# Mamba-2 layer of a two-layer trunk: the step-size chain's stacked operand is written in place, and the hold on group 0's convolutions starts later in the group and ends later in the chain

## The chip, the cores and the metric

The kernel runs on one core of one Trainium2 chip. TensorE (PE, the matmuls), VectorE (DVE), ScalarE (ACT), GpSimd (POOL) and SyncE (SP, which here only issues transfers) each work through a queue of their own in order. An instruction that must wait for another engine holds up everything behind it in its queue. The metric is the device time of one execution in microseconds.

## The reference, cut to what matters

The step runs a gated-MLP layer, a Mamba-2 layer and an MLP after each, on 256 prompt rows and 8 sequences of 8 rows (320 columns in the kernel). The change lies in the Mamba-2 mixer:

```python
zxbcdt = h @ w_in                                  # 6144 columns and 32 for dt
conv = conv_b + xp[:, 0:l] * conv_w[0]
for k in range(1, CONV_W):
    conv = conv + xp[:, k:k + l] * conv_w[k]
xbc_c = jax.nn.silu(conv)                          # gives x, B, C
dt = jax.nn.softplus(dt_raw + dt_bias)             # 32 heads
a = -jnp.exp(a_log)
...
acum = jnp.cumsum(dt * a, axis=2)                  # within a chunk
seg = acum[:, :, :, None] - acum[:, :, None, :]
decay = jnp.exp(jnp.where(causal, seg, -jnp.inf))
...
decay_to_end = jnp.exp(acum[:, :, -1:] - acum)
```

Every head needs `acum`, `dt` and `dt * decay_to_end` before its state-space work (the "ssd" below) can start.

## The kernel before, in words

Everything is feature-major: 128 partitions by 320 columns. Each projection tile (128 output features) takes 24 matmuls on PE: 8 blocks of the contraction, three products each (lines 307 to 309), since both operands are split into a high and a low part. A weight tile arrives by a transfer of SP's queue (`raw`, line 147), ACT makes its high part (`whi`, line 136) and DVE its low part (`wlo`, line 137). `whi` and `wlo` have three buffers each, so the fourth `whi` waits until PE has finished with the first. The results lie in three PSUM buffers, `mm`: a fourth tile can't start before ACT has read the first.

The Mamba-2 layer has eight groups. A group has six projection tiles: B, C, two tiles of x (here Xa, Xb) and two of the gate z (Za, Zb). B, C, Xa and Xb go through a convolution (`conv`): ACT copies the PSUM tile into `cb` (lines 640 and 641), POOL fills in and saves the borders (638, 639, 642, 643), ACT makes the first tap `co` (646), DVE adds the other three (649), and ACT applies Silu (651, 652). `cb` and `co` have three buffers each. Then comes the group's `ssd`: transposes and small matmuls on PE (lines 681 to 735), Y (757), the states (794), with the decay matrix `bc` made on ACT (687, 688) from rows that a transfer spreads over the partitions.

Ahead of group 0 stands the dt chain (lines 819 to 860), on the columns of `w_dt`, which are repeated four times over the partitions: softplus by a series on DVE (823 to 832), the running sum (835, 836), its exponentials on ACT (838, 841, 844), and a stacked operand `stk` whose four quarters of 32 partitions hold `acum`, `dt`, `dt` times the decay to the chunk's end, and `dt`. POOL writes `stk` in four instructions (845 to 848). PE transposes `stk` (854, 859) into `nat`, which every `ssd` needs, and SP writes `acum` and its exponential to DRAM (850, 851) and reads them back spread over the partitions (673, 674).

The order within each queue is set by a scheduler that runs when the kernel is built and that places instructions by costs of its own; the code's order is only a start. `tc.issue_after(i)` tells it that what stands under it must not be placed before `i`. With it, the three DVE taps of group 0's convolutions are held until the running sum (`dtl[0]`); `dtl` is cleared after group 0's convolutions, so later groups are never held. `widx` counts the projection tiles of the groups: within `conv` it is 1 for group 0's B, 2 for C, 3 for Xa, 4 for Xb.

Of the kernel before, what the change touches and what calls it, by code (L numbers as in the profile page):

```python
# [12 lines left out]
ADD, SUB, MUL, MIN, MAX = ALU.add, ALU.subtract, ALU.mult, ALU.min, ALU.max  # L13
# [9 lines left out]
T = TP + TS  # L23
# [22 lines left out]
C_ID, C_SS, C_S4, C_MASK, C_RST, C_DM, C_SEL, C_M = 0, 128, 138, 174, 494, 814, 1070, 1102  # L46
# [6 lines left out]
def tile_trunk(ctx: ExitStack, tc: tile.TileContext, io):  # L53
    nc = tc.nc
    pe, act, dve, pool = nc.tensor, nc.scalar, nc.vector, nc.gpsimd
# [12 lines left out]
    def nm(s):  # L68
        uid[0] += 1
        return f"{s}{uid[0]}"  # L70

    cst = const.tile([P, C_N], F32, name="cst")
# [546 lines left out]
    yst = [yp.tile([P, 8, T], F32, tag=f"yst{i}", name=f"yst{i}", bufs=1) for i in range(2)]  # L619
# [4 lines left out]
    widx = [0]  # L624
    dtl = []

    def in_tile():
        i = widx[0]
        widx[0] += 1
        if i < MG - 1:  # L630
            return scaled(pss[1 + i], r0)
        return proj_h(io["w_in"][i])

    def conv(ct, tag, bufs):
        ps = in_tile()
        cb = mb.tile([P, CW], F32, tag="cb", name=nm("cb"), bufs=3)
        cs = cb[:, 3 + TP :].rearrange("p (b t) -> p b t", t=11)
        pool.memset(cb[:, 0:3], 0.0)
        pool.tensor_copy(cs[:, :, 0:3], scv[:, ct])
        act.copy(cb[:, 3 : 3 + TP], ps[:, :TP])  # L640
        act.copy(cs[:, :, 3:], b1(ps[:, TP:T]))
        pool.tensor_copy(cvp[:, ct, :], cb[:, TP : TP + 3])
        pool.tensor_copy(scv[:, ct], cs[:, :, 8:])
        o = mb.tile([P, CW], F32, tag="co", name=nm("co"), bufs=3)
        wv = lambda k: vec[:, V_CW + ct * 4 + k : V_CW + ct * 4 + k + 1]
        act.activation(o[:, :CO], cb[:, :CO], AF.Identity, scale=wv(0), bias=vec[:, V_CB + ct : V_CB + ct + 1])  # L646
        with tc.issue_after(dtl[0]) if dtl else ExitStack():
            for k in range(1, 4):
                dve.scalar_tensor_tensor(o[:, :CO], cb[:, k : k + CO], wv(k), o[:, :CO], MUL, ADD)  # L649
        r = mb.tile([P, T], F32, tag=tag, name=nm(tag), bufs=bufs)  # L650
        act.activation(r[:, :TP], o[:, :TP], AF.Silu)
        act.activation(b1(r[:, TP:]), o[:, 3 + TP :].rearrange("p (b t) -> p b t", t=11)[:, :, 0:8], AF.Silu)
        return r
# [150 lines left out]
    def convs(g_, prev):  # L804
        B = conv(16 + g_, "Bt", 2)
        next(prev, None)
        C = conv(24 + g_, "Ct", 2)
        next(prev, None)
        X = []
        for r in range(2):  # L810
            X.append(conv(2 * g_ + r, "Xt", 4))
            next(prev, None)
        Z = mt([P, 2, T], "Z", 2)
        for r in range(2):
            act.activation(Z[:, r], in_tile()[:, :T], AF.Silu)
            next(prev, None)
        return B, C, X, Z

    raw, dt, acm, stk, t1, t2, t3 = (yst[1][:, i, :] for i in range(7))
    act.activation(raw, ps[:, :T], AF.Identity, bias=vec[:, V_DTB : V_DTB + 1])  # L820
    act.activation(t1, raw, AF.Abs)
    act.activation(t1, t1, AF.Exp, scale=-1.0)
# [10 lines left out]
    na = mb.tile([P, 1], F32, name="na")  # L833
    act.activation(na, vec[:, V_AL : V_AL + 1], AF.Exp)
    dve.tensor_scalar(t1, dt, na, -1.0, MUL, MUL)
    dtl.append(dve.tensor_tensor_scan(acm, cst[:, C_RST : C_RST + T], t1, 0.0, MUL, ADD).ins)
    eac = raw
    act.activation(eac, acm, AF.Exp)
    for c in range(2):
# [2 lines left out]
    a8 = b1(acm[:, TP:])  # L842
    dve.tensor_tensor(b1(t3[:, TP:]), a8[:, :, LS - 1 : LS].to_broadcast([P, NB, LS]), a8, SUB)
    act.activation(t2[:, TP:], t3[:, TP:], AF.Exp)
    pool.tensor_copy(stk[0:32], acm[0:32])
    pool.tensor_copy(stk[32:64], dt[32:64])
    pool.tensor_tensor(stk[64:96], dt[64:96], t2[64:96], MUL)
    pool.tensor_copy(stk[96:128], dt[96:128])
    rowd = dr.tile([2, NH, T], F32, name="rowd")
    nc.sync.dma_start(rowd[0], acm[0:32, :])  # L850
    nc.sync.dma_start(rowd[1], eac[0:32, :])
# [257 lines left out]
```

## Time and profile before

| | |
|---|---|
| median of 3 runs | 1079.7 us (1076.17 to 1083.86) |
| the profiled execution's own time | 1075.66 us |
| its span in the trace | 1073.9 us |
| mean granted TensorE clock | 0.986 of full speed |
| busy share: PE, DVE, ACT, POOL | 96%, 61%, 51%, 28% |
| dt chain's place in the span | 510 to 541 us |
| Mamba-2 groups' place in the span | 509 to about 790 us |

The span is shorter than the execution by 1.8 us. The busy shares are means over a span whose stages differ, so they say what the kernel is made of and not what a change in the dt chain is worth; for that one looks at the stretch in which the chain runs. The page divides the span into 40 slices of 26.8 us; slices 20 and 21 hold the chain.

### The profile page before, as it was taken

Reading aid. Unit: us, or ns where it says so; the run is one execution under the profiler, and the core shown is the slowest. Engines: PE = TensorE matmul, PEld = TensorE weight load, DVE = VectorE, ACT = ScalarE, POOL = GpSimd, SP = SyncE. Lnnn points to the kernel's source line nnn. Section 1 sums busy time; section 2 is a strip of 40 time slices with the busy share of each in tenths; the row PEclk is TensorE's granted clock in tenths of the full one; section 3 lists DMA queues with packets and bytes.
Section 4 is the critical chain, followed back from the end, with each engine's and each line's share of the span. In section 5 each row is a group of like instructions: output and inputs, shape, how many; then the busy total and the mean of one; then the engine's idle time right before and its main releaser. Section 6 shows DMA issues by size and latency. Waiting matters only on the chain.

```text
span 1073.9 us, 19747 instructions
## 1 busy us (share of the span) xinstructions
PE 1030.2 (96%) x7809; PEld 970.8 (90%) x7809; DVE 652.9 (61%) x1080; ACT 549.2 (51%) x1013; POOL 299.9 (28%) x403
## 2 busy tenths in 40 slices
PE   5999999999999999999688999999999999999996
PEld 3778998999999999999688999999999999999995
DVE  4545966437644443446968898898876754444432
ACT  4453343435644433335698777678345555543331
POOL 1200134332433311222123333532217243411001
PEclk9999999999999999999888999999999999999998
DMA  9957985775666667455435656565445544544431
GB/s 366 361 194 237 335 316 166 267 253 195 243 215 216 217 223 271 151 157 172 151 108 171 251 168 222 197 224 205 167 163 158 177 157 140 155 153 144 155 99 50
DMA packets 60877, 213.97 MB, mean 199 GB/s; under 512 B 6560, under 2 KB 12128, under 8 KB 58480
## 3 DMA queue, kind: packets, MB, share of 16 engines
q1 hardware_dynamic: 58544, 200.47, 55.1%
q0 software_dynamic: 1952, 11.98, 3.1%
q8 instruction: 61, 1.00, 0.4%
q10 hardware_dynamic: 288, 0.26, 0.1%
q14 instruction: 32, 0.26, 0.1%
HBM read 199.31 MB, written 12.85 MB: 198 GB/s over the span
## 4 chain that ended last, share of the span: by engine, by line
PE 76%; ACT 7%; DVE 6%; issue 5%; DMA 3%; POOL 2%; SPq 0%; POOLq 0%; ACTq 0%; DVEq 0%
PE mm L307 19%; PE mm L308 19%; PE mm L309 19%; PE adap L165 3%; ACT bc L687 2%; DMA bc<-rowd 2%; DVE wlo L137 2%; DVE co L649 2%; ACT whi L136 1%; PE mm L411 1%; PE mm L412 1%; PE mm L413 1%; PE ax L757 1%; DMA raw<-ada 1%; PE ax L307 1%
## 5 line engine op out<-in xcount | busy, mean ns | idle before, releaser
L137 DVE TENSOR_TENSOR wlo<-raw,whi 128x1024 fp32r<-128x1024 f32 (+1 forms) x243 | 298.1, 1228 | 203.5 <-ACT whi L136 202.6
L136 ACT ACTIVATE whi<-raw 128x1024 fp32r<-128x1024 f32 (+1 forms) x243 | 254.7, 1050 | 252.4 <-PE mm L308 195.0
L307 PE MATMUL mm<-hhi,whi 128*128 128x320 f32 x952 | 300.1, 316 | 1.9 <-ACT ta L356 0.9
L308 PE MATMUL mm<-hlo,whi 128*128 128x320 f32 x952 | 296.8, 313 | 0.1
L309 PE MATMUL mm<-hhi,wlo 128*128 128x320 f32 x952 | 296.9, 313 | 0.0
L307 PEld LDWEIGHTS mm<-hhi,whi 128*128 128x128 f32 x952 | 180.2, 190 | 7.5 <-issue 3.3
L308 PEld LDWEIGHTS mm<-hlo,whi 128*128 128x128 f32 x952 | 180.1, 189 | 1.9 <-DVE hlo L267 1.0
L309 PEld LDWEIGHTS mm<-hhi,wlo 128*128 128x128 f32 x952 | 180.0, 189 | 1.4 <-DVE mv L198 0.4
L307 PE MATMUL mm<-mhi,whi 128*128 128x320 f32 x512 | 158.3, 309 | 0.0
L308 PE MATMUL mm<-mlo,whi 128*128 128x320 f32 x512 | 158.1, 309 | 0.0
L309 PE MATMUL mm<-mhi,wlo 128*128 128x320 f32 x512 | 158.0, 309 | 0.0
L358 POOL TENSOR_TENSOR ta<-ta 128x320 f32<-128x320 f32 x64 | 82.0, 1285 | 140.0 <-ACT ta L356 118.2
L307 PEld LDWEIGHTS mm<-mhi,whi 128*128 128x128 f32 x512 | 96.1, 188 | 1.2 <-issue 0.8
L308 PEld LDWEIGHTS mm<-mlo,whi 128*128 128x128 f32 x512 | 96.1, 188 | 0.0
L309 PEld LDWEIGHTS mm<-mhi,wlo 128*128 128x128 f32 x512 | 96.1, 188 | 0.0
L293 POOL TENSOR_TENSOR x<-x,rs 128x64 f32<-128x64 f32 x28 | 11.2, 399 | 218.5 <-DVE rs L292 218.5
L359 ACT ACTIVATE mhi<-ta 128x320 fp32r<-128x320 f32 x64 | 30.1, 471 | 81.9 <-POOL ta L358 81.6
L360 DVE TENSOR_TENSOR mlo<-ta,mhi 128x320 fp32r<-128x320 f32 x64 | 33.5, 523 | 59.2 <-ACT mhi L359 59.2
L649 DVE SCALAR_TENSOR_TENSOR co<-cb,vec,co 128x344 f32<-128x344 f32 x96 | 54.7, 585 | 6.1 <-ACT co L646 5.9
L165 PE MATMUL adap<-ara,sc 128*32 128x256 f32 x640 | 43.0, 383 | 0.0
L307 PE MATMUL mm<-uhi,whi 128*128 128x320 f32 x128 | 40.0, 315 | 0.0
L308 PE MATMUL mm<-ulo,whi 128*128 128x320 f32 x128 | 40.0, 315 | 0.0
(340 smaller groups left out, 1691.8 us busy)
## 6 DMA issues: line engine op xcount, KB each, us to landing
raw<-mlp_w SPq DMA_DIRECT2D x128, 512.0 KB, 3.6
ara<-ada_w SPq DMA_DIRECT2D x80, 512.0 KB, 6.3
raw<-w_in SPq DMA_DIRECT2D x48, 512.0 KB, 3.7
raw<-ada SPq DMA_DIRECT2D x16, 512.0 KB, 9.9
raw<-gm_wv SPq DMA_DIRECT2D x16, 512.0 KB, 8.7
raw<-gm_wu SPq DMA_DIRECT2D x16, 512.0 KB, 5.8
raw<-gm_wo SPq DMA_DIRECT2D x16, 512.0 KB, 5.3
st<-state SPq DMA_DIRECT2D x8, 1024.0 KB, 5.5
```

Source lines behind the costliest of these rows:

```text
L136: act.activation(hi[:, :n], raw[:, :n], AF.Copy)
L137: eng.tensor_tensor(lo[:, :n], raw[:, :n], hi[:, :n].bitcast(F32), SUB)
L165: pe.matmul(ps[32 * j : 32 * j + 32, :256], lhsT=sc[:, kb + i, :], rhs=rs[i][:, j * 256 : (j + 1) * 256], start=(kb + i == AB - 1), stop=( ...
L293: (dve if m == KD - 1 else pool).tensor_tensor(x[:, m, TP:], x[:, m, TP:], t0, ADD)
L307: pe.matmul(ps[:, :n], lhsT=whi[:, kk, :], rhs=hi, start=first, stop=False)
L308: pe.matmul(ps[:, :n], lhsT=whi[:, kk, :], rhs=lo, start=False, stop=False)
L309: pe.matmul(ps[:, :n], lhsT=wlo[:, kk, :], rhs=hi, start=False, stop=last)
L358: pool.tensor_tensor(s, t, t, MUL)
L359: act.activation(mhi[:, m, :], s, AF.Copy)
L360: dve.tensor_tensor(mlo[:, m, :], s, mhi[:, m, :].bitcast(F32), SUB)
L649: dve.scalar_tensor_tensor(o[:, :CO], cb[:, k : k + CO], wv(k), o[:, :CO], MUL, ADD)
L687: act.activation(bc[:, h, cq[c]], bc[:, h, cq[c]], AF.Relu, bias=nat[:, c, HG * g_ + h : HG * g_ + h + 1], scale=-1.0)
```

## The change

Three edits. First, `stk` is no longer a tile of its own: it is `dt` itself. Two quarters already hold `dt`; ACT overwrites the first with `acum` (line 846 of the changed kernel), and DVE multiplies the third by the decay to the chunk's end in place (line 847). POOL does nothing in the chain any more. Second, the hold ends at that DVE product and no longer at the running sum. Third, group 0's B and C are not held at all, only Xa and Xb are.

```diff
--- before.py
+++ after.py
@@ -644,7 +644,7 @@
         o = mb.tile([P, CW], F32, tag="co", name=nm("co"), bufs=3)
         wv = lambda k: vec[:, V_CW + ct * 4 + k : V_CW + ct * 4 + k + 1]
         act.activation(o[:, :CO], cb[:, :CO], AF.Identity, scale=wv(0), bias=vec[:, V_CB + ct : V_CB + ct + 1])
-        with tc.issue_after(dtl[0]) if dtl else ExitStack():
+        with tc.issue_after(dtl[0]) if dtl and widx[0] > 2 else ExitStack():
             for k in range(1, 4):
                 dve.scalar_tensor_tensor(o[:, :CO], cb[:, k : k + CO], wv(k), o[:, :CO], MUL, ADD)
         r = mb.tile([P, T], F32, tag=tag, name=nm(tag), bufs=bufs)
@@ -816,7 +816,8 @@
             next(prev, None)
         return B, C, X, Z
 
-    raw, dt, acm, stk, t1, t2, t3 = (yst[1][:, i, :] for i in range(7))
+    raw, stk, acm, t1, t2, t3 = (yst[1][:, i, :] for i in range(6))
+    dt = stk
     act.activation(raw, ps[:, :T], AF.Identity, bias=vec[:, V_DTB : V_DTB + 1])
     act.activation(t1, raw, AF.Abs)
     act.activation(t1, t1, AF.Exp, scale=-1.0)
@@ -833,7 +834,7 @@
     na = mb.tile([P, 1], F32, name="na")
     act.activation(na, vec[:, V_AL : V_AL + 1], AF.Exp)
     dve.tensor_scalar(t1, dt, na, -1.0, MUL, MUL)
-    dtl.append(dve.tensor_tensor_scan(acm, cst[:, C_RST : C_RST + T], t1, 0.0, MUL, ADD).ins)
+    dve.tensor_tensor_scan(acm, cst[:, C_RST : C_RST + T], t1, 0.0, MUL, ADD)
     eac = raw
     act.activation(eac, acm, AF.Exp)
     for c in range(2):
@@ -842,10 +843,8 @@
     a8 = b1(acm[:, TP:])
     dve.tensor_tensor(b1(t3[:, TP:]), a8[:, :, LS - 1 : LS].to_broadcast([P, NB, LS]), a8, SUB)
     act.activation(t2[:, TP:], t3[:, TP:], AF.Exp)
-    pool.tensor_copy(stk[0:32], acm[0:32])
-    pool.tensor_copy(stk[32:64], dt[32:64])
-    pool.tensor_tensor(stk[64:96], dt[64:96], t2[64:96], MUL)
-    pool.tensor_copy(stk[96:128], dt[96:128])
+    act.copy(stk[0:32], acm[0:32])
+    dtl.append(dve.tensor_tensor(stk[64:96], stk[64:96], t2[64:96], MUL).ins)
     rowd = dr.tile([2, NH, T], F32, name="rowd")
     nc.sync.dma_start(rowd[0], acm[0:32, :])
     nc.sync.dma_start(rowd[1], eac[0:32, :])
```

The lines of the chain shift by one (823 becomes 824 and so on up to 844, which becomes 845), and `tile` numbers shift by two. Since the scheduler places everything anew, the queues change from here to the end of the layer. Three places follow. In the names, `co_`, `cb_` and `mm_` numbers belong to one tile each: in the changed kernel 5357, 5378, 5399 and 5420 are `co` of group 0's B, C, Xa and Xb; 5537, 5603, 5665 and 5734 are `co` of group 1's B, C, Xa and Xb; `mm_5499`, `5565`, `5627`, `5696`, `5754`, `5840` are group 1's six projection tiles B, C, Xa, Xb, Za, Zb, and `mm_5921` is group 2's B.

DVE's queue of the kernel before, from the series to the end of the running sum and the first held taps (`yst` is the chain's storage; `co_5359`, `5380` and `5401` are group 0's B, C and Xa):

```order
L829 SCALAR_TENSOR_TENSOR yst_5250<-yst_5250 128x320 x4
L137 TENSOR_TENSOR wlo_5760<-raw_5757,whi_5759 128x1024
L829 SCALAR_TENSOR_TENSOR yst_5250<-yst_5250 128x320 x3
L137 TENSOR_TENSOR wlo_5846<-raw_5843,whi_5845 128x1024
L830 TENSOR_SCALAR yst_5250<-yst_5250 128x320
L831 TENSOR_TENSOR yst_5250<-yst_5250 128x320
L832 SCALAR_TENSOR_TENSOR yst_5250<-yst_5250 128x320
L835 TENSOR_SCALAR yst_5250<-yst_5250,na 128x320
L836 SCALAR_TENSOR_TENSOR yst_5250<-cst,yst_5250 128x320
L649 SCALAR_TENSOR_TENSOR co_5359<-cb_5352,vec,co_5359 128x344
L649 SCALAR_TENSOR_TENSOR co_5380<-cb_5373,vec,co_5380 128x344
L649 SCALAR_TENSOR_TENSOR co_5401<-cb_5394,vec,co_5401 128x344
```

The same place of DVE's queue in the changed kernel, up to the running sum (line 837):

```order
L649 SCALAR_TENSOR_TENSOR co_5537<-cb_5530,vec,co_5537 128x344
L830 SCALAR_TENSOR_TENSOR yst_5250<-yst_5250 128x320
L137 TENSOR_TENSOR wlo_5925<-raw_5922,whi_5924 128x1024
L830 SCALAR_TENSOR_TENSOR yst_5250<-yst_5250 128x320
L649 SCALAR_TENSOR_TENSOR co_5603<-cb_5596,vec,co_5603 128x344
L831 TENSOR_SCALAR yst_5250<-yst_5250 128x320
L649 SCALAR_TENSOR_TENSOR co_5603<-cb_5596,vec,co_5603 128x344
L832 TENSOR_TENSOR yst_5250<-yst_5250 128x320
L649 SCALAR_TENSOR_TENSOR co_5603<-cb_5596,vec,co_5603 128x344
L833 SCALAR_TENSOR_TENSOR yst_5250<-yst_5250 128x320
L836 TENSOR_SCALAR yst_5250<-yst_5250,na 128x320
L837 SCALAR_TENSOR_TENSOR yst_5250<-cst,yst_5250 128x320
```

Before, no tap stood between the series' start and the running sum; now twelve do: three each of group 0's B and C (ahead of these rows) and of group 1's B and C, which no hold ever covered, and one more `wlo`. Group 1's Xa follows the sum (three taps), then the product of line 847, then group 0's Xa and Xb.

PE's queue of the kernel before, from the last matmul of group 1's Xa (`mm_5629` there) to the first of its Xb (`mm_5698`):

```order
L309 MATMUL mm_5629<-hhi,wlo_5633 128x320
L854 MATMUL ax_5329<-cst,yst_5250 128x128 x3
L859 MATMUL ax_5336<-cst,dup_5334 128x128 x2
L697 MATMUL adap_5619<-cst,Bt_5364 128x128 x2
L681 MATMUL ax_5547<-Ct_5385,Bt_5364 128x128 x2
L681 MATMUL ax_5547<-Ct_5385,Bt_5364 128x64
L307 MATMUL mm_5698<-hhi,whi_5701 128x320
```

The same place in the changed kernel (of each tile the first or the last matmul):

```order
L309 MATMUL mm_5627<-hhi,wlo_5631 128x320
L697 MATMUL adap_5617<-cst,Bt_5362 128x128 x2
L307 MATMUL mm_5696<-hhi,whi_5699 128x320
...
L307 MATMUL mm_5754<-hhi,whi_5757 128x320
...
L309 MATMUL mm_5840<-hhi,wlo_5844 128x320
L853 MATMUL ax_5327<-cst,yst_5250 128x128 x3
L307 MATMUL mm_5921<-hhi,whi_5924 128x320
```

Three whole projection tiles now stand ahead of the chain's transposes (line 854 before, 853 now), which stood first.

ACT's queue in the changed kernel, between the preparation of weights and the chain's exponentials (lines 839 to 846):

```order
L136 ACTIVATE whi_5924<-raw_5922 128x1024
L651 ACTIVATE Bt_5542<-co_5537 128x256
L652 ACTIVATE Bt_5542<-co_5537 128x64
L640 COPY cb_5596<-mm_5565 128x256
L641 COPY cb_5596<-mm_5565 128x8x8
L646 ACTIVATE co_5603<-cb_5596,vec 128x344
L651 ACTIVATE Ct_5608<-co_5603 128x256
L652 ACTIVATE Ct_5608<-co_5603 128x64
L640 COPY cb_5658<-mm_5627 128x256
L641 COPY cb_5658<-mm_5627 128x8x8
L646 ACTIVATE co_5665<-cb_5658,vec 128x344
L839 ACT_TABLE_LOAD
```

And the kernel before at the chain's exponentials:

```order
L136 ACTIVATE whi_5845<-raw_5843 128x1024
L838 ACT_TABLE_LOAD
L838 ACTIVATE yst_5250<-yst_5250 128x320
L841 ACTIVATE yst_5250<-yst_5250 128x128 x2
L844 ACTIVATE yst_5250<-yst_5250 128x64
L613 COPY dup_5334<-yst_5250 128x256
L651 ACT_TABLE_LOAD
```

Group 1's B and C and the emptying of three PSUM tiles have moved ahead of the exponentials. Over the whole program ACT has 25 table loads in place of 27.

## Rows read from the trace of the kernel before

**Rows 1.** The page, section 2: PE busy in 40 slices of the span, in tenths.

```profile
PE   5999999999999999999688999999999999999996
```

**Rows 2.** Busy us by engine (instructions) in stretches; then PEclk, DMA share, GB/s.

```profile
530.00:540.00 10.00, 2.58 (x9) 1.78 (x10) 8.50 (x16) 5.45 (x16) 4.59 (x13) 0.56 0.64 208
540.00:550.00 10.00, 10.00 (x57) 9.99 (x56) 6.13 (x11) 9.98 (x35) 1.55 (x10) 0.75 0.27 86
550.00:560.00 10.00, 8.22 (x56) 7.86 (x55) 6.05 (x8) 9.96 (x22) 1.02 (x4) 1.00 0.18 54
560.00:570.00 10.00, 7.13 (x119) 6.71 (x118) 7.90 (x13) 9.94 (x19) 2.31 (x8) 0.94 0.54 183
570.00:580.00 10.00, 10.00 (x50) 8.89 (x50) 10.00 (x12) 9.39 (x21) 4.70 (x4) 0.72 0.31 94
```

**Rows 3.** PE in order of time: start, us, what [idle before <-releaser].

```profile
536.37 0.90 PE L854 MATMUL ax<-cst,yst 128*128 128x128 f32 x3 [8.10 <-POOL yst L847]
...
541.69 0.47 PE L307 MATMUL mm<-hhi,whi 128*128 128x320 f32 x1
541.96 0.47 PE L308 MATMUL mm<-hlo,whi 128*128 128x320 f32 x1
...
546.67 0.31 PE L307 MATMUL mm<-hhi,whi 128*128 128x320 f32 x1
...
549.61 0.31 PE L309 MATMUL mm<-hhi,wlo 128*128 128x320 f32 x1
...
552.57 1.13 PE L735 MATMUL ax<-xe,Bn 128*128 128x256 f32 x4 [1.78 <-ACT Bn L701]
...
561.41 0.44 PE L757 MATMUL ax<-cp,S 128*64 128x128 f32 x4
...
567.87 0.38 PE L794 MATMUL ax<-xst,Bst 32*128 32x256 f32 x1 [2.87 <-DVE xst L729]
```

**Rows 4.** DVE in order of time: the chain and the held taps.

```profile
520.91 1.23 DVE L137 TENSOR_TENSOR wlo<-raw,whi 128x1024 fp32r<-128x1024 f32 x1 [0.52 <-ACT whi L136]
...
523.33 1.23 DVE L137 TENSOR_TENSOR wlo<-raw,whi 128x1024 fp32r<-128x1024 f32 x1 [0.95 <-ACT whi L136]
524.48 2.07 DVE L829 SCALAR_TENSOR_TENSOR yst<-yst 128x320 f32<-128x320 f32 x4
...
532.22 0.95 DVE L836 TENSOR_TENSOR_SCAN yst<-cst,yst 128x320 f32<-128x320 f32 x1
533.10 1.86 DVE L649 SCALAR_TENSOR_TENSOR co<-cb,vec,co 128x344 f32<-128x344 f32 x3
```

**Rows 5.** ACT in order of time, after the chain's exponentials.

```profile
536.77 1.28 ACT L651 ACT_TABLE_LOAD   x1
538.07 0.42 ACT L651 ACTIVATE Bt<-co 128x256 f32<-128x256 f32 x1
...
539.44 0.35 ACT L640 COPY cb<-mm 128x256 f32<-128x256 f32 x1
...
542.54 3.41 ACT L687 ACTIVATE bc<-bc,nat 128x128 f32<-128x128 f32 x12
...
550.99 1.27 ACT L688 ACTIVATE bc<-bc 128x1280 f32<-128x1280 f32 x1
...
558.39 1.05 ACT L136 ACTIVATE whi<-raw 128x1024 fp32r<-128x1024 f32 x1
```

**Rows 6.** POOL in order of time: the last write of the stacked operand.

```profile
535.46 0.85 POOL L847 TENSOR_TENSOR yst<-yst 32x320 f32<-32x320 f32 x1 [1.37 <-ACT yst L844]
```

**Rows 7.** PE in steps of 1 us: busy, granted clock, DMA.

```profile
551.00:552.00 1.00, 0.00 (x0) 1.00 0.00 0
...
569.00:570.00 1.00, 1.00 (x6) 0.50 0.24 97
```

**Rows 8.** All engines in the later groups, columns as in Rows 2.

```profile
600.00:770.00 170.00, 166.13 (x1520) 160.27 (x1520) 154.02 (x274) 125.14 (x275) 64.10 (x98) 1.00 0.57 195
```

## The prediction

> **What bounds the kernel now.** The slices come first [rows 1]: PE is at nine tenths or more nearly everywhere, so PE's queue sets the end, and only the stretches where PE idles or runs at half clock can give time back. Such a dip stands in slices 19 to 21. Next the stretches around it [rows 2]: from 530 to 540 PE has 2.58 us of work, from 550 to 570 it lacks 1.8 and 2.9 us, and the clock averages 0.56, 0.75, 0.94 and 0.72 of full speed in four of the five. Third, PE in order of time names the waits [rows 3]: it has nothing for 8.1 us until, at 536.37, the stacked operand is there (line 854); 1.8 us at line 735; 2.9 us at line 794. After 8.1 us without work the clock is at 1.2 GHz and matmul starts are 0.27 us apart, where they are 0.147 us apart at 2.4 GHz (20 steps from 546.67 to 549.61) [rows 3].
>
> Why did PE have nothing to do at 528? The projection tile that could follow needs a PSUM buffer, ACT empties it into a `cb`, and all three `cb` wait for the held taps, which start at 533.10, just after the running sum [rows 4]. So the hold bought an early dt chain with PE's idle time. A full projection tile is 24 x 0.147 = 3.53 us.
>
> **The change part by part.** I walk the new queues with the old durations, from 528.3, where PE stops in the old trace (536.37 less 8.10). Steps: a tap 0.6, a `wlo` 1.15 (523.33 to 524.48), a series step 0.5 [rows 4]; on ACT a `whi` 1.0, a table load 1.28, the exponential of line 688 1.27, twelve decay steps of line 687 3.4 [rows 5]. ACT's other short steps go by the mean of 540 to 550, 9.98 us for 35 or 0.285 each [rows 2]; a Silu or a copy into `cb` is two of them, and the rows of 0.42 and 0.35 for the longer half [rows 5] let me say 0.5.
>
> POOL's part. The last POOL write takes 0.85 us [rows 6]. In its place DVE does one product on 32 partitions (a series step of the same 320 columns takes 0.5 [rows 4], POOL's own 0.85 is the upper bound; I take 0.5), and ACT one copy of about 0.4, by the 0.35 for 256 columns [rows 5]. Between the sum's end at 533.15 and POOL's last write at 535.46 lie 2.3 us in which ACT waits for a short DVE product; the copy goes there. So this part is worth 0.35 us on the chain (0 to 0.35), and nothing at the end unless PE waits for the chain. The other three POOL writes lay beside the exponentials and gain nothing.
>
> The chain gets later. Twelve taps (7.2 us) and one `wlo` (1.15) enter DVE's queue ahead of the running sum; 1.5 us of this fills waits for `whi` that stand there now, 0.52 and 0.95 [rows 4]. The sum moves from 533.15 to about 540.0. The same 2.3 us behind it give 542.3, the product 542.8. The transposes, at 536.37 before [rows 3], come at 542.9.
>
> PE is filled meanwhile. With group 0's B and C free, `cb` buffers turn over. Group 1's Xb needs the buffer of B, emptied at about 528: it runs from 528.7 to 532.2. Za needs that of C. ACT stands at `whi_5924`, which waits for Xb's weights to be done with (532.2); then `whi` 1.0, Silu of B 0.5, the copy 0.5: Za runs from 534.1 to 537.6, after 1.9 us of idle. Zb needs the buffer of Xa, which needs C's three taps (they alternate with the series and end at 537.7), a Silu and a copy: 538.7 to 542.2, 1.1 us idle. The transposes then wait 0.7 and take some 0.7 (0.9 at half clock in the row); group 2's B waits for the copy of Xb, which stands behind a `whi`, a table load and the Silu of Za after ACT's last exponential (542.3): 545.3, 1.7 us idle. So by 545.3 PE has idled 5.4 us instead of 8.1 and has three tiles behind it, at full clock if the gaps don't lower it.
>
> The wait that is late next. From 545.3 PE has three tiles (B, C, Xa of group 2) and some 1.6 us of transposes and small products, five pieces at 0.3 as one transpose of line 854's row [rows 3]: until 557.5. The next weights, `whi_6121`, stand on ACT behind all of group 0's and group 1's decay steps. From the copy of `nat` at 547.6: 24 steps of line 687 6.8, load and exponential 2.55, three Silu 1.5, two PSUM copies 1.0, six short copies 1.7, two first taps 1.2 (as DVE's taps), together 14.7: 562.3, `whi_6121` 563.3, and its `wlo`, behind two taps on DVE, 565.2. Of the 7.7 us until then PE fills some 2.1, 1.1 of it with line 735 [rows 3] and the rest with lines 713, 717 and four matmuls: it idles 5.6. Then 38 matmuls (5.6 us) and Y (line 757, 3.6 us, from 561.41 to 565.0 in the old trace [rows 3]) follow without a wait that I find: 574.4.
>
> **The sum.** At 574.4 the new kernel has done group 0's Y and 7.75 tiles since 528.3. The old one has done the same Y at 565.0 but only 4.08 tiles. The other 3.67 cost 12.9 us; ahead of them it still has its wait of 2.9 and its second stretch at half clock: 0.28 of 10 us and 0.06 of 10 us below full clock [rows 2] are 3.4 us lost. That makes 584.2, so the change leads by 9.8 us.
>
> Two deductions. The pieces from 557.5 to 565.2 leave PE mostly idle, in gaps of 1 us or less. For the clock the nearest rows are a gap of 1.8 us after which it still stands at full (row 551) and one of 2.9 us after which it is at half (row 569) [rows 7]: between 0 and 3.4 us, I take half, 1.7. And the groups that follow: from 600 to 770 DVE is busy 154 of 170 us and PE 166 [rows 8]. The ssd work of group 0 ends at nearly the same time as before, with more tiles ahead of it; by the end of the layer the two queues agree again, so DVE has to do the rest in some 10 us less, 0.96 of the time. What PE waits for it then lies between 0 (all of it hidden, and perhaps 3 of PE's 3.9 idle us won) and all of the lead; I take 2. The forecast is 9.8 - 1.7 - 2 = 6 us faster: 1069.7 against the profiled execution's 1075.66, and 1074 against the median of 1079.7, which lies 4.0 above that execution.
>
> A rule on table loads weighs on the walk. Row first: the load at 536.77 takes 1.28 us and the Silu behind it starts at 538.07, 0.02 us after its end [rows 5]. The Trainium skill ("ScalarE: Activation LUTs", What ACT_TABLE_LOAD costs) gives 1.28 us for the load and about 1.38 us for a drain with it. By that the three loads between the sum and `whi_6121` would cost an estimated 4.1 us more, and the forecast would be about 2 us faster than before; the rows show no such drain, and I go by them.
>
> **The rivals.** First, *all of the lead holds*: the gaps leave the clock up and DVE has room, which 16 us of idle in 600 to 770 speak for. 9.8 us, and up to 3 of PE's idle time there: 1067 to 1070. Second, *the wait moves*: the chain is 6.5 us later, and ACT, at 9.9 of 10 us from 540 to 570 already [rows 2], is the engine that PE waits for. If `whi_6121` is 4 us later than in my walk, or the later groups don't make up for group 0's late ssd, the gain is eaten: 1078 to 1082. Third, *the clock stays low*, which makes the kernel slower: if it falls in the first gap, at 532 to 534, and doesn't rise until the dense run after 565, then 6.75 tiles x 24 x 0.12 us = 19 us, and some 6 us of small matmuls take twice as long; of these 25 us about 8.5 lie in gaps, 16.5 come on top, and 9.8 are won: 7 us slower, 1087. It decides from about 20 us of work at half clock outside the gaps on. The row of 1.8 us at full clock speaks against it [rows 7]. It is the course that the Trainium skill ("TensorE: Matmul & The Clock Gate", A second HAM failure mode: psum-queue depth-cycling) describes: short pauses of PE at every turn of its PSUM buffers, after which the clock swings and throughput falls. Fourth, *it doesn't do what it says*: the hold is meant to bring the last product forward and the new order puts more in front of it. That is in the sum; were PE to need the product at once, as in the old order, it would cost 6.5 us and no tile would fill it, 1086.
>
> **How the numbers follow.** My forecast (1070 to 1078) gets 0.5, the full lead 0.2, the moved wait 0.2, low clock and unfilled wait together 0.1. The range, 1065 to 1082, leaves out the slow ones and a rest. About 1% (10.8 us) is what a measurement of this kernel can tell from no change: faster by more than that has most of the full lead's chance, 0.2, slower by more than that the far end of the slow cases, 0.05, the rest is within.
>
> **What would show it.** In the new trace: PE without the gap of 8.1 us, with gaps of 1 to 2 us near 533, 538 and 544; the running sum at 539 to 541; line 853 at 542 to 544; a longer sparse stretch near 558 to 565 that ends at `whi` or `wlo`; no wait of 2.9 us at line 794. Wrong would be: a granted clock of 0.5 over more than 10 us after 532, a sum later than 543, or new idle time of PE over 6 us between 600 and 770.

## The result and the profile after

The changed kernel takes 1086.2 us (median of 11 runs, 1083.3 to 1093.2), the kernel before 1079.4 us (11 runs, 1076.2 to 1083.9). The ratio is 1.0065, with a 95% interval of 1.0047 to 1.0083: some 7 us slower, where 6 us faster was forecast. Twice more beside the kernel before, it gave 1.0044 and 1.0058.

In the profiled execution of the changed kernel the layer begins 2.86 us later than before, at 511.44 us (the first projection product of the layer; 508.58 before), ahead of everything that the change touches. Times of the new trace are therefore compared less 2.86. Two more profiles of the same kernel were taken later; they are called its second and third execution. The slices of the page answer to [rows 1]: the dip at slice 20 is gone, smaller ones have come behind it.

```profile
PE   5999999999999999999979999999899999999996
PEclk9999999999999999999999979999999999999998
```

The stretches around the change, busy us by engine (instructions) and then the clock, answer to [rows 2]. Even with that shift, TensorE now works from 530 to 560 25.4 of 30 us at full clock, where it had 20.8 at 0.56 to 1.00.

```profile
530.00:540.00 10.00, 8.18 (x56) 7.91 (x55) 9.56 (x19) 5.57 (x15) 2.62 (x10) 1.00 0.64 193
540.00:550.00 10.00, 7.81 (x54) 7.04 (x52) 8.15 (x15) 9.82 (x23) 2.01 (x7) 1.00 0.48 155
550.00:560.00 10.00, 9.38 (x66) 9.10 (x65) 3.69 (x6) 9.97 (x33) 2.24 (x6) 1.00 0.48 171
560.00:570.00 10.00, 7.14 (x29) 5.47 (x30) 9.04 (x14) 9.98 (x21) 3.07 (x7) 0.84 0.21 60
...
600.00:650.00 50.00, 48.22 (x418) 44.61 (x415) 41.01 (x73) 31.38 (x71) 18.25 (x28) 0.86 0.57 187
...
600.00:770.00 170.00, 161.56 (x1477) 152.36 (x1473) 144.58 (x262) 113.52 (x252) 64.24 (x93) 0.95 0.56 185
```

TensorE in order of time in the changed kernel answers to [rows 3]. The gap of 8.10 us is gone. In its place stand gaps of 1.82, 0.38 and 1.63 us, and further on 1.18 and 0.93 (the longest; smaller ones are left out). Group 0's Y (line 757) ends at 577.1, and behind it line 794 follows without the old wait of 2.87 us.

```profile
536.68 0.41 PE L307 MATMUL mm<-hhi,whi 128*128 128x320 f32 x1 [1.82 <-ACT cb L641]
...
544.81 0.55 PE L853 MATMUL ax<-cst,yst 128*128 128x128 f32 x3 [0.38 <-DVE yst L847]
546.99 0.41 PE L307 MATMUL mm<-hhi,whi 128*128 128x320 f32 x1 [1.63 <-ACT Z L815]
...
560.56 0.44 PE L717 MATMUL ax<-cst,dup 128*128 128x128 f32 x2 [1.18 <-ACT dup L613]
...
564.79 0.41 PE L307 MATMUL mm<-hhi,whi 128*128 128x320 f32 x1 [0.93 <-ACT whi L136]
...
577.22 0.38 PE L794 MATMUL ax<-xst,Bst 32*128 32x256 f32 x1
```

On VectorE the running sum ends at 541.31, and the product that replaces GpSimd's takes 0.48 us ([rows 4] and [rows 6] have the same place before).

```profile
540.48 0.83 DVE L837 TENSOR_TENSOR_SCAN yst<-cst,yst 128x320 f32<-128x320 f32 x1
...
544.28 0.48 DVE L847 TENSOR_TENSOR yst<-yst 32x320 f32<-32x320 f32 x1 [0.99 <-ACT yst L845]
```

So up to 580 the change does what the walk of the queues said. Yet the layer (from its first projection product to the first product of the block that follows) takes 328.8 us instead of 317.5, and 323.5 and 325.2 in the second and third execution; what follows the layer, up to TensorE's last product, takes 239 to 240 us in all four. The loss lies in the groups behind group 0. There is one profile of the kernel before, of an execution 3.7 us below its median, while the three of the changed kernel lie 1.0 to 3.4 us above theirs. So the layers' differences, 6 to 11 us, are larger than those of the medians, 4 to 7, and the shares read from these traces below are not exact for a typical execution. In the row for 600 to 770, TensorE is busy 161.56 us where it was busy 166.13 [rows 8]. The clock of 0.86 in 600 to 650 comes from one stretch of 13.7 us at half clock that the second and third execution don't have.

### The profile page after: what moved, and what is told of

Read it like the earlier page. It is cut to its first block, busy times and chain, and to the rows that moved or that the text cites. A ratio compares the mean times of both kernels' runs of the same rounds, so it can differ in the third digit from the quotient of the medians.

```text
span 1087.8 us, 19733 instructions
## 1 busy us (share of the span) xinstructions
PE 1040.3 (96%) x7809; PEld 976.9 (90%) x7809; DVE 652.3 (60%) x1081; ACT 546.4 (50%) x1012; POOL 303.8 (28%) x399
## 4 chain that ended last, share of the span: by engine, by line
PE 76%; ACT 7%; DVE 5%; issue 4%; DMA 4%; POOL 3%; SPq 0%; POOLq 0%; ACTq 0%; DVEq 0%
PE mm L307 19%; PE mm L308 19%; PE mm L309 19%; PE adap L165 3%; ACT bc L687 2%; DMA bc<-rowd 2%; ACT whi L136 1%; PE ax L757 1%; DVE wlo L137 1%; PE mm L411 1%; DVE co L649 1%; PE mm L412 1%; PE mm L413 1%; POOL Y L769 1%; DMA raw<-ada 1%
## 5 line engine op out<-in xcount | busy, mean ns | idle before, releaser
L307 PEld LDWEIGHTS mm<-hhi,whi 128*128 128x128 f32 x952 | 181.9, 191 | 19.2 <-ACT Z L815 7.9
L687 ACT ACTIVATE bc<-bc,nat 128x128 f32<-128x128 f32 (+1 forms) x96 | 28.1, 371 | 26.2 <-DMA bc<-rowd 26.2
L769 POOL TENSOR_TENSOR Y<-Y,Z 128x640 f32<-128x640 f32 x8 | 33.8, 4226 | 24.9 <-DVE Y L768 24.8
```

Source lines behind the costliest of these rows:

```text
L307: pe.matmul(ps[:, :n], lhsT=whi[:, kk, :], rhs=hi, start=first, stop=False)
L687: act.activation(bc[:, h, cq[c]], bc[:, h, cq[c]], AF.Relu, bias=nat[:, c, HG * g_ + h : HG * g_ + h + 1], scale=-1.0)
L769: pool.tensor_tensor(Y, Y, Z, MUL)
```

## The experiments

The theories at the start were four: A, the lead of some 10 us is won and lost again in the groups that follow; B, the new way of building the stacked operand costs; C, the later end of the hold costs; D, any order of the later groups other than that of the kernel before costs, whatever the lead is. "Free" tiles are those whose taps are not held.

**The chain in place, nothing else** (all four tiles held until the running sum, as before):

```diff
-    raw, dt, acm, stk, t1, t2, t3 = (yst[1][:, i, :] for i in range(7))
+    raw, stk, acm, t1, t2, t3 = (yst[1][:, i, :] for i in range(6))
+    dt = stk
-    pool.tensor_copy(stk[0:32], acm[0:32])   # and three more GpSimd writes
+    act.copy(stk[0:32], acm[0:32])
+    dve.tensor_tensor(stk[64:96], stk[64:96], t2[64:96], MUL)
```

> The kernel before with the stacked operand written in place (ACT copy, DVE product) and nothing else: all four of group 0's convolutions stay held, until the running sum. Theory A (the time is lost after the chain: the freed tiles win about 10 us up to group 0's Y, and the later groups lose more than that in waits of PE and in stretches at half clock): here no tile is freed, so the ratio to before is 0.997 to 1.003, and the chain's transposes come 0.3 to 0.7 us earlier behind the running sum than the 3.2 us of before. Theory B (the new form of the chain itself costs the time, a DVE product behind taps and an ACT copy in place of POOL): ratio 1.004 to 1.008.

Measured 1.0012 [0.9993, 1.0032] (the ratio to the kernel before, here and below, with its 95% interval): no difference. B falls. The chain was expected to get shorter by 0.3 to 0.7 us and got longer: 3.61 us from the end of the running sum to the transposes, where the kernel before has 3.20 (3.51 in the changed kernel). In this kernel three held taps (1.54 us) stand ahead of the new product on VectorE; in the changed kernel ScalarE's copy (line 846) stands ahead of the last exponential (line 845), for which the product waits 0.99 us.

**In place, all four tiles held until the last product:**

```diff
-    dtl.append(dve.tensor_tensor_scan(acm, cst[:, C_RST : C_RST + T], t1, 0.0, MUL, ADD).ins)
+    dve.tensor_tensor_scan(acm, cst[:, C_RST : C_RST + T], t1, 0.0, MUL, ADD)
-    dve.tensor_tensor(stk[64:96], stk[64:96], t2[64:96], MUL)
+    dtl.append(dve.tensor_tensor(stk[64:96], stk[64:96], t2[64:96], MUL).ins)
```

> In place, and the hold ends at the DVE product, but all four of group 0's convolutions are held. Theory A: nothing is freed, PE waits for the chain as before, now about 0.5 us less; the taps start some 2 us later than at the running sum; ratio 0.997 to 1.004. Theory C (the later end of the hold costs the time): ratio 1.004 or more, with taps some 2.5 us later behind the sum.

Measured 1.0088 [1.0062, 1.0113]. What TensorE waits for between 520 and 560 us in this kernel (total us, how often, longest):

```profile
PE adap L697 <- ACT Bt L651: 7.6, 1, 7.6
PE ax L853 <- DVE yst L847: 6.9, 1, 6.9
```

The wait for the chain (line 853) is only 1.5 us shorter than the 8.4 us of the kernel above, and a second of 7.6 us follows (line 697), for B itself, since the held taps now start behind the product. With everything held, a later end of the hold is dear; whether it is with two tiles free is tested below.

**Two tiles free, GpSimd's chain, hold until the running sum:**

```diff
-        with tc.issue_after(dtl[0]) if dtl else ExitStack():
+        with tc.issue_after(dtl[0]) if dtl and widx[0] > 2 else ExitStack():
```

> The kernel before with POOL's chain and the hold until the running sum, only B and C of group 0 are not held. In its order the transposes stand behind 3.75 more projection tiles. Theory A: the 8.1 us wait of PE at the transposes is gone, group 0's Y comes with a lead of 7 to 11 us of PE work, and it is lost later: ratio 1.000 to 1.010. Theories B and C: without the other two edits the lead remains, ratio 0.990 to 0.996.

Measured 1.0045 [1.0022, 1.0069]. This one line alone has a loss of the same size. Beside it the changed kernel again:

> The changed kernel once more, for a second profile. Theory A: the running sum, the transposes and group 0's Y within 1 us of the first profile when counted from the dt tile's first matmul, and again more than 15 us at half clock between group 0's Y and the end of the layer. If the half-clock stretch of 13.7 us at 635 to 649 was a chance of that one execution, it is absent here and the layer is 5 to 7 us shorter than in the first profile.

Measured 1.0044 [1.0019, 1.0069]. Its layer loses 12.4 us to TensorE's idle time and half clock in the first 80 us, where the one of before loses 22.3, and then 14.3 us, where the one of before loses 4.0 (gaps between TensorE's rows, plus half of the busy time inside stretches at half clock).

**Less lead or more.** Group 1's convolutions held as well (the list of holds is cleared only after group 1), with the hold until the product and, in the second kernel, until the running sum; then no hold at all; then the changed kernel with taps from group 2 on kept behind the Y of the group two earlier:

```diff
         prev = ssd(g_, *ld, *cz)
-    dtl.clear()                  # ahead of the loop over the groups
+        dtl.clear()              # after group 1
```

> The changed kernel with the hold extended to all four convolutions of group 1 (the list of held points is cleared after group 1 and no longer after group 0). In its order six taps and no longer twelve stand ahead of the running sum, one projection tile and no longer three stands ahead of the chain's transposes, and from group 1 on the small products stand at the same tiles as in the kernel before. Theory A (a lead of several tiles makes the ssd work lag, and the later groups lose it in waits, half clock and split-up small products): the lead is only 2 to 4 us, but it is kept; the later groups cost PE no more than before; ratio 0.993 to 1.000. Theory D (any order other than that of before costs in the later groups, whatever the lead): ratio 1.003 or more.

```diff
+    dtl.append(dve.tensor_tensor_scan(acm, cst[:, C_RST : C_RST + T], t1, 0.0, MUL, ADD).ins)
-    dtl.append(dve.tensor_tensor(stk[64:96], stk[64:96], t2[64:96], MUL).ins)
+    dve.tensor_tensor(stk[64:96], stk[64:96], t2[64:96], MUL)
```

> As the run before, but the hold ends at the running sum and not at the DVE product. Theory A: as that run, and 1 to 2 us less, since the held taps start earlier; ratio 0.991 to 0.999. Theory D: 1.003 or more.

```diff
-        with tc.issue_after(dtl[0]) if dtl and widx[0] > 2 else ExitStack():
+        with ExitStack():
```

> The changed kernel with no convolution held at all. In its order the chain's transposes stand behind nearly nine projection tiles and 28 taps stand ahead of the running sum. Theory A: PE's waits before the transposes are nearly gone, so the lead at the transposes is the largest of all, and group 0's ssd lags most; more is lost later: idle and half clock behind group 0's Y above those of the changed kernel (11 us idle, 14 to 20 us at half clock), ratio 1.004 to 1.02. Were the lead worth anything at the end, the ratio would be below 1.

```diff
+        lead = ydone.get(cur[0] - 2) if cur[0] >= 2 else None   # the Y of the group two earlier
+        with tc.issue_after(lead) if lead is not None else (...):
```

> The changed kernel, and from group 2 on a group's taps may not stand before the Y of the group two before it. The chain is as in the changed kernel, and the small products of group 1 stand one tile earlier. Theory A: the dt stretch is unchanged (group 0's Y within 1 us of the changed kernel), PE has less lead for the later groups, and little of the loss goes: ratio 1.000 to 1.008, and 1.000 to 1.003 if the length of the lead alone decides.

Measured 1.0063 [1.0035, 1.0091], 1.0041 [1.0022, 1.0060], 1.0065 [1.0044, 1.0086] and 1.0052 [1.0030, 1.0073]. Without a hold TensorE idles 1.2 us in the first 40 us of its layer instead of 10.3, the largest lead of all, and the end is no better. Idle time and half clock, in the first 80 us of the layer and behind them, are 24.6 and 16.5, 20.4 and 13.0, 11.8 and 19.2, 16.7 and 11.8 us in these four. So the two with group 1 held have little lead or none at 80 us, less than the 2 to 4 us expected, and lose as much later. A's step "less lead, less loss" falls; all four fit D, which says nothing yet of the place.

**One place.** Added up in steps of 40 us, the three profiled executions of the changed kernel share one loss that the one of before has not: 3.2 to 3.6 us of idle time and a stretch of 3.4 us at half clock, some 250 us into the layer. ScalarE in order of time there, first in the kernel before:

```profile
749.32 1.18 ACT L873 ACTIVATE hhi<-yst 128x320 fp32r<-128x320 f32 x3
...
753.35 1.79 ACT L873 ACTIVATE hhi<-yst 128x320 fp32r<-128x320 f32 x4 [1.96 <-PE mm L309]
755.04 1.04 ACT L136 ACTIVATE whi<-raw 128x1024 fp32r<-128x1024 f32 x1
755.99 0.42 ACT L815 ACTIVATE Z<-mm 128x320 f32<-128x320 f32 x1
756.31 0.46 ACT L873 ACTIVATE hhi<-yst 128x320 fp32r<-128x320 f32 x1
760.41 0.74 ACT L774 ACTIVATE Z<-Y 128x640 f32<-128x640 f32 x1 [3.65 <-POOL Y L769]
```

and in the changed kernel (its third execution):

```profile
757.39 2.21 ACT L872 ACTIVATE hhi<-yst 128x320 fp32r<-128x320 f32 x5
765.03 0.74 ACT L774 ACTIVATE Z<-Y 128x640 f32<-128x640 f32 x1 [5.44 <-POOL Y L769]
765.68 0.81 ACT L872 ACTIVATE hhi<-yst 128x320 fp32r<-128x320 f32 x2
766.39 1.04 ACT L136 ACTIVATE whi<-raw 128x1024 fp32r<-128x1024 f32 x1
767.34 0.41 ACT L815 ACTIVATE Z<-mm 128x320 f32<-128x320 f32 x1
767.66 0.46 ACT L872 ACTIVATE hhi<-yst 128x320 fp32r<-128x320 f32 x1
```

Line 774 squares group 6's Y and waits for GpSimd's product of Y and Z, 6.0 us long before and 6.4 in the changed kernel. In both kernels ScalarE stands there. Before, all eight rows `hhi` of the output projection (the expectation below says seven), its weights and the last Z are ahead of the wait; in the changed kernel three of the eight rows, the weights and Z are behind it. TensorE has come to the output projection, which takes these rows as they arrive (in the second execution the longer of its two waits, 1.9 us, is for the row's low part `hlo` and 1.3 us for Z):

```profile
762.02 0.41 PE L308 MATMUL mm<-hlo,whi 128*128 128x320 f32 x1 [0.69 <-DVE hlo L873]
767.81 0.41 PE L307 MATMUL mm<-hhi,whi 128*128 128x320 f32 x1 [2.88 <-ACT Z L815]
772.33 0.78 PE L681 MATMUL ax<-Ct,Bt 128*128 128x128 f32 x6
```

and after the 2.88 us the clock falls (steps of 1 us; behind the engines stand clock, DMA share and GB/s):

```profile
766.00:767.00 1.00, 0.00 (x0) 0.00 (x0) 1.00 (x3) 1.00 (x3) 0.00 (x0) 1.00 0.00 0
...
769.00:770.00 1.00, 1.00 (x6) 1.00 (x5) 1.00 (x2) 0.00 (x0) 0.21 (x1) 0.50 0.00 0
```

That is theory E: 2.9 to 3.6 us of waiting and 1.7 us lost to half clock, 3 to 5 us in all, come from one instruction's place on ScalarE. The test moves that instruction alone:

```diff
-        act.activation(q0, Y, AF.Square)
+        with tc.issue_after(zl[0]) if g_ == NG - 2 else ExitStack():   # zl: the last Z copy
+            act.activation(q0, Y, AF.Square)
```

> The changed kernel with one order fixed: ScalarE may square group 6's Y (line 774 of the changed kernel) only behind the copy of the last Z of group 7. Computes the same. In the changed kernel ScalarE stands 5.4 to 5.7 us at that square, waiting for GpSimd's product, with three of the eight hhi rows, a weight copy and the last Z behind it; in the kernel before it waits there too, but with seven of the eight rows, the weights and Z ahead. TensorE, which has reached the output projection and takes it row by row, waits 3.2 to 3.6 us for those rows and runs 3.4 us at half clock. Theory E (this place costs the changed kernel 3 to 5 us): ratio to the kernel before 1.000 to 1.003, and in the profile less than 2 us of TensorE idle from 240 to 290 us after the layer's first product. Theory D (the loss is spread over all later groups and one place gives nothing at the end): 1.004 to 1.007.

Measured 1.0032 [1.0008, 1.0057], just above E's range and below D's; in the profile TensorE idles 1.9 us from 240 to 290 us after the layer's first product, as E said. Two kernels put the product of Y and Z of group 6 on VectorE instead, in the changed kernel and in the kernel before:

```diff
-        pool.tensor_tensor(Y, Y, Z, MUL)
+        (dve if g_ == NG - 2 else pool).tensor_tensor(Y, Y, Z, MUL)
```

> The changed kernel with the product of Y and Z of group 6 alone on VectorE in place of GpSimd, where it takes some 6 us. Computes the same. The square behind it then finds its input early, wherever it stands. Theory E: the 5.4 us of ScalarE idle at group 6's square go, ratio to the kernel before 0.999 to 1.003. Theory D: 1.004 to 1.007.

> The kernel before with the same product of group 6 on VectorE. Computes the same. ScalarE waits 3.6 us at that square in the kernel before, but TensorE does not wait in that stretch. Theory E, by which only the rows behind the square matter: 0.999 to 1.001. Were the GpSimd product itself a limit in both kernels, 0.995 to 0.998.

Measured 1.0048 [1.0027, 1.0069] and 1.0028 [1.0008, 1.0048]: both above what E said, and the first where D had it. In its profile ScalarE's wait at the square did shrink, from 5.44 to 0.70 us. The control is slower too, so this edit has a price of its own, some 3 us, that I had not foreseen; if it is the same in both kernels, which was not shown, the first agrees with the moved square. By itself this pair doesn't decide between D and E. What the price is, with 0.81 us of VectorE added and 6 us of GpSimd removed, these runs don't tell. The last kernel of this series has both the moved square and a hold until the running sum, the edit of the sum shown above:

> The changed kernel with two edits: the hold ends at the running sum again, as in the kernel before, and the square of group 6 stands behind the last Z. Group 0's B and C stay free, the stacked operand is built in place. Computes the same. Theory E with a small price for the late end of the hold: 0.997 to 1.001, the best of all orders tried. Theory D: 1.003 to 1.006, as with the first two tiles free and the old stacked operand (1.0045).

Measured 1.0010 [0.9992, 1.0027], no difference from the kernel before that could be seen. Since it confounds two edits, they were crossed on one chip, each edit as in the diffs above:

> The changed kernel, to stand beside three others of the same run that differ from it in one or two edits: whether the hold ends at the last product or at the running sum, and whether ScalarE's square of group 6's Y stands where the scheduler put it or behind the last Z. It has the product and the scheduler's place. 1.0045 to 1.0065 to the kernel before, as measured twice.

> The changed kernel with the square of group 6 behind the last Z, once more. Theory E (the place costs the changed kernel 3 to 5 us): at least 0.0020 below the changed kernel of this run, 1.001 to 1.0035. Theory D (the loss lies in all later groups): within 0.0015 of it.

> The changed kernel with the hold ended at the running sum, and the square of group 6 where the scheduler puts it, which is further forward still: ahead of six of the eight rows of the output projection instead of three. If the end of the hold alone makes the kernel with both edits as fast as before (1.0010): 1.000 to 1.002. If the square does: 1.0035 to 1.006.

> Both edits, once more: 1.000 to 1.002 to the kernel before; if the two add up, it is below the changed kernel by the sum of what each gives alone.

| ratio to the kernel before | square where it was put | square behind the last Z |
|---|---|---|
| hold until the product | 1.0058 [1.0040, 1.0077] | 1.0020 [1.0000, 1.0039] |
| hold until the running sum | 1.0058 [1.0034, 1.0082] | 1.0022 [1.0007, 1.0037] |

Down a column nothing changes: with two tiles free the end of the hold costs nothing that shows, and C falls. Along each row the moved square gives 0.0036 to 0.0038, 4 us. The two kernels on the right are the same as those measured above at 1.0032 and 1.0010, so from one series to the next the same kernel differs by 0.0012, and some 0.002 of the loss is left in both. ScalarE and TensorE in the kernel with the square moved (line numbers are three or four higher; first ScalarE, then TensorE):

```profile
758.83 2.63 ACT L875 ACTIVATE hhi<-yst 128x320 fp32r<-128x320 f32 x7
761.37 1.04 ACT L136 ACTIVATE whi<-raw 128x1024 fp32r<-128x1024 f32 x1
762.32 0.41 ACT L818 ACTIVATE Z<-mm 128x320 f32<-128x320 f32 x1
767.31 0.74 ACT L777 ACTIVATE Z<-Y 128x640 f32<-128x640 f32 x1 [4.58 <-POOL Y L771]
```

```profile
763.47 0.41 PE L308 MATMUL mm<-hlo,whi 128*128 128x320 f32 x1 [1.90 <-DVE hlo L876]
769.29 0.78 PE L683 MATMUL ax<-Ct,Bt 128*128 128x128 f32 x6
```

ScalarE still waits 4.58 us, but only one row stands behind it. TensorE's wait of 2.88 us is gone, the other is 1.90 instead of 0.69, and the first product of group 7's ssd (line 681, here 683) comes 3 us earlier (769.29 against 772.33, both layers having begun at 511.7). No order beat the kernel before.

## Why the prediction was wrong

**The walk was right.** Less 2.86, the running sum ended at 538.5 (forecast 540.0), the transposes began at 542.0 (542.9), Y ended at 574.2 (574.4). From 531.1 to 577.2 TensorE started 185 projection products, 7.7 tiles, where the sum had 7.75. The writes in place were worth nothing at the end (in_place), as forecast, though the chain got 0.3 us longer by them and not 0.35 shorter. That Y came within 0.2 us is in part luck: TensorE idled 4.0 us (1.82, 0.18, 0.38 and 1.63) where the walk gives 5.4, and 3.5 in the sparse stretch where it gives 5.6; half clock and products that took longer than in the walk made up for that. The lead 80 us into the layer, as the difference in idle time and half clock up to there, is 22.3 less 12.4 to 13.0 in the three executions, 9.3 to 9.9 us. The sum had 9.8, and 8.1 less its term for the clock, which the measured figure contains. Counted by products done it is 60 more of the projections (8.8 us) and four fewer of line 735 (0.9 us), some 8 us.

**The clock** was a term of 1.7 us, and one stretch of 3.4 us at half clock, which costs those 1.7 us, came where it was expected, after the sparse stretch (0.84 in the row for 560 to 570); it was 6.8 us long in the third execution. The low clock of the third rival didn't come there.

**The step that failed is the second of the two deductions**, "the groups that follow". I took 2 us, with bounds of nothing and all of the lead. Measured, it is all of the lead, 8 to 10 us, and 5 to 7 us more: some 15 us in the place of 2. Two things were wrong in it. First, I costed the later groups by their amounts: VectorE busy 154 of 170 us [rows 8], so at most the lead could be given back. The bound held only if the later queues kept their order, and they don't: the scheduler writes every queue anew when one tile moves. Second, I counted ahead only to Y of group 0. Stretches of the layer in the kernel before, from its first product (80, 160 and 50 us):

```profile
508.58:588.58 80.00, 65.04 (x466) 61.21 (x465) 65.31 (x107) 67.80 (x152) 18.64 (x53) 0.87 0.43 137
588.58:748.58 160.00, 156.13 (x1452) 149.81 (x1451) 143.88 (x262) 117.70 (x261) 62.70 (x101) 1.00 0.62 215
748.58:798.58 50.00, 50.00 (x478) 46.99 (x475) 41.23 (x77) 21.47 (x40) 12.67 (x9) 1.00 0.43 157
```

the same of the changed kernel (third execution):

```profile
511.73:591.73 80.00, 70.35 (x519) 65.17 (x517) 68.64 (x112) 67.14 (x154) 25.10 (x52) 0.96 0.48 155
591.73:751.73 160.00, 152.94 (x1375) 145.02 (x1376) 136.29 (x254) 113.72 (x256) 63.29 (x97) 0.98 0.58 202
751.73:801.73 50.00, 46.43 (x445) 42.98 (x444) 38.81 (x70) 20.13 (x37) 12.45 (x7) 0.97 0.35 117
```

and with the square moved (second execution):

```profile
511.72:591.72 80.00, 70.79 (x519) 66.07 (x517) 68.62 (x112) 67.17 (x154) 25.09 (x52) 0.96 0.48 155
591.72:751.72 160.00, 154.36 (x1373) 146.12 (x1374) 134.94 (x253) 112.38 (x252) 61.62 (x95) 0.97 0.59 200
751.72:801.72 50.00, 48.10 (x469) 44.97 (x468) 42.55 (x78) 22.54 (x42) 15.28 (x12) 1.00 0.42 144
```

In the first 80 us the changed kernel gains 5.3 us of TensorE's work and most of the half clock. In the next 160 it loses 3.2 us of work and 0.02 of the clock, another 3.2 us. In the last 50 it loses 3.6 us and 0.03, 1.5 us, where the kernel before has no idle time at all. This last is the square, and it is the one part that an edit took back, for the most part: with the square moved the last 50 us still have 1.9 us of idle time. The middle part is spread over waits of 1 to 2 us; the longest sums by what was waited for, from 588 us to the layer's end, in the kernel before and then in the changed one (third execution):

```profile
PE nrm L205 <- DVE nv L199: 2.0, 2, 1.3
PE adap L713 <- DVE Bst L704: 1.3, 2, 1.0
PE nrm L210 <- DVE ta L776: 0.6, 1, 0.6
```

```profile
PE mm L307 <- ACT Z L815: 4.9, 2, 2.9
PE nrm L210 <- DVE ta L776: 2.1, 2, 1.5
PE nrm L205 <- DVE nv L199: 2.1, 2, 1.5
PE adap L713 <- DVE Bst L704: 1.8, 1, 1.8
```

The two for Z are the place above and one of 2.0 us at 592. That one may be of the same sort: ScalarE stands 2 to 3 us at group 0's square, ahead of the Z copy, but 8.6 us of other ScalarE work with two table loads lie between the two, and no run moved that square. The rest is in busy time, with half clock counted as half, added over TensorE's rows in the layer: 291.2 us before, 296.3 to 296.8 in the three executions, for the same products in other pieces between the tiles. The layer's difference then adds up: in the third execution 9.3 us won in the first 80 us, 11.6 lost to idle time and half clock behind them, 5.4 to longer busy time, together the 7.7 us by which the layer is longer. The longer busy time is not what the slow orders share: with two tiles free alone it is 290.5 us, with the hold until the running sum 292.5, and both are as slow, by idle time and half clock (15.0 and 12.2 us of them behind the first 80). So only the square's share, 4 of those 15 us, is shown by an experiment, and what causes the rest stays open.

**Rivals.** "The wait moves" named the right kind, a wait on ScalarE with the later groups not making up for it, but in the wrong place (`whi_6121`) and with a limit of 1082 that the measured 1086 passed. "The clock stays low" gave nearly the right time by a mechanism that didn't happen. Of the signs set down in advance, two of the three gaps, the sparse stretch and the missing 2.9 us came; the middle gap was 0.18 us, and the running sum (538.5) and line 853 (542.0) came at or just ahead of the early ends of their stretches. The sign for wrong, over 6 us of new idle time of TensorE between 600 and 770, stood at its edge: 4.6 in the profiled execution (161.56 against 166.13), 3.8 and 6.4 in the other two.

## What to carry to other kernels

A lead that a change wins early is worth what the rest of the program lets TensorE keep; read the last stretch in which TensorE never waits, and ask which instruction of another engine would stand ahead of its operands if TensorE came there at another time. Where a scheduler writes the queues, an edit of one early constraint is an edit of all later queues, and the amounts of work don't bound what that costs. A long product on another engine (6 us on GpSimd) is harmless until a blocking instruction that waits for it stands ahead of something that TensorE needs: put that instruction behind by hand.

## What was not expected of the hardware

The granted clock fell after waits as short as these, with sparse work between them: in the profiled execution of the changed kernel TensorE's gaps of 1.18, 0.43, 0.36, 0.93 and 0.39 us between 560 and 566 were followed by 3.4 us at half clock, while the gaps of 1.82 and 1.63 us at 536 and 546, with dense work between, were not. The stretches at half clock in the layer were 3.4 to 17.1 us long, and the long ones differ from execution to execution of one kernel: 13.7 us with TensorE busy in the first profile of the changed kernel, none over 6.8 in the two others. The same product of Y and Z, 128 x 640, takes GpSimd 3.54 us in group 0 and 6.42 in group 6 of the changed kernel (3.53 and 6.02 before; 3.51 in group 6 of in_place), and VectorE 0.81 us. In group 6 of the changed kernel it runs beside long VectorE work (lines 785, 745 and 873); that this slows it was not tested. In in_place, where GpSimd's product takes 3.51 us, it is line 745 on VectorE beside it that takes longer, 2.30 us instead of 0.94. GpSimd in order of time in the changed kernel, third execution:

```profile
578.65 3.54 POOL L769 TENSOR_TENSOR Y<-Y,Z 128x640 f32<-128x640 f32 x1 [1.24 <-DVE Y L768]
...
758.58 6.42 POOL L769 TENSOR_TENSOR Y<-Y,Z 128x640 f32<-128x640 f32 x1 [3.85 <-DVE Y L768]
```
